# Hybrid streaming encoder on one core: memory values with tokens on partitions, a priority for the output projection, another slot for the last rows of x

## The chip, the cores and the metric

The kernel runs on one core of a Trainium2 chip. Its time is the device time of one launch in microseconds (us). TensorE (PE in the profile) multiplies, VectorE (DVE) and ScalarE (ACT) do elementwise work and read PSUM, GpSimd (POOL) does a little elementwise work, and SyncE (SP) issues nearly all DMAs, in the order of its own queue. Each engine works through its instructions in an order that is fixed when the kernel is built.

## What is computed

One layer of an encoder, for 1024 prompt tokens and 64 sample tokens, D = 1024:

- h = RMSNorm(x) @ W_in, split into the inputs of four mixers: a convolution of 31 taps over 256 channels, two kinds of softmax-like attention (`fox`, `sb`; 4 heads of 64 each) and a recurrence (`hgrn`).
- x += concat(convolution, fox, hgrn, sb) @ W_out.
- x += attention of 4 heads over 256 memory tokens, whose keys and values are made here: `mk = mem_prompt @ w_mk`, `mv = mem_prompt @ w_mv` (256 x 1024 by 1024 x 1024 each; both are outputs too).
- x += relu(RMSNorm(x) @ W_up)^2 @ W_down, then a last RMSNorm.

Activations and weights are float32. Each product is made as three products of float32r parts: a high part times a high part, high times low, low times high.

## The kernel before

**Layout.** Activations are kept with features on partitions and tokens in columns. A weight tile of 128 output columns is loaded as 8 blocks of 128 x 128 (`fetch_w`, L177: 512 KB), split on ScalarE into a high part `wh` and on VectorE into a low part `wl` (`split`, L169), and is the stationary operand of 8 x 3 products per chunk of tokens (`mm3`, L188). Tokens come in chunks of 512, 256 and 320 columns in the first stage (`CH`, L215) and in two groups afterwards (`GR`, L216): group 0 is tokens 0 to 511, group 1 the other 576, in chunks of 320 and 256.

**Preamble (L244 to L293).** The rows of x arrive as nine tiles `xt0` to `xt8` (L252); the ninth holds x_sample. TensorE transposes them in three rounds into `px`, from which the parts of h are made (`hx`, `ap`), and `stats` (L259) makes the scale `rb` of each token. The tiles xt7 and xt8 stand in slots that attention uses later: xt7 in that of `vn`, xt8 in that of `kT`.

**Mixing stage (L296 to L1032).** Four generators ("lanes") emit instructions: the projections with W_in, attention, convolution, recurrence. The loop at L1016 takes turns among them, and each lane has a priority: `PR_PROJ`, `PR_ATT`, `PR_HGRN`, `PR_CONV`, in this order from first to last. A scheduler sets the order on each engine when the kernel is built: among the instructions that it takes to be ready it puts the one with the lowest priority number first. The products of the projections have the priority `PR_MM` (`products`, L322), later than all lanes, so that they fill what attention leaves of TensorE. The first lane follows `PROJ_ORDER` (L40); it begins with the first pair of `sb` heads, whose key is written into `kT` by `sink_k` (L439) and whose value goes through `sink_v` (L444). Sums are made in a pool of two PSUM banks (`ps_mm`, tag `mm`).

**Memory keys and values (`memory_kv`, L373)** are the last step of the first lane. The memory tokens are transposed into `mT`, split, and for each of the 8 tiles of 128 weight columns of w_mk and of w_mv one sum of 24 products with the 256 tokens as columns is made. `sink` (L389) copies it out (`mkvT`), for the keys stores it, transposes it back in two products (`pn`), copies that (`mnat`) and stores it with tokens in rows.

**Convolution (`lane_conv`, L758).** Three chunks of tokens, the last one from token 752 on. Its 31 taps for two halves of the channels are VectorE instructions (L794); then come mean and variance by products with ones (`pme`, `pva`), a normalization and a sigmoid, in two halves, and stores into `mix_d`.

**Output projection.** After the lanes the priority is `PR_END` (L1033). The eight mixer rows of group 0 are loaded into slots of `kT`, `vn` and `q2` (L1043 to L1047) and split (`split_mix`, L1035); then the pools of the mixing stage close. `dense_add(0, w_out, ...)` (L1227) runs over 8 weight tiles with 24 products of 512 columns each (`pa`) and adds the sums to `xt` (L1120). Its hook `ahead` (L1219) loads x and, at the second weight tile, loads and splits the eight mixer rows of group 1, convolution last. `rms_apply` makes h for group 0, and `dense_add(1, ...)` projects group 1, taking mixer rows 2 to 7 first and the convolution's rows 0 and 1 last (`MIX`, L1226). Memory attention, the feed-forward part and the last norm follow; the change does not touch them.

Of the kernel before, what the change touches and what calls it, by code (L numbers as in the profile page):

```python
# [8 lines left out]
F32 = mybir.dt.float32  # L9
F32R = mybir.dt.float32r  # L10
BF16 = mybir.dt.bfloat16
U8 = mybir.dt.uint8
AF = mybir.ActivationFunctionType
# [4 lines left out]
P = 128  # L18
D = 1024
KD = D // P  # L20
SP = 1024
SS = 64
T = SP + SS
# [5 lines left out]
NMEM = 256  # L29
# [9 lines left out]
P_COST = 18.0  # L39
PROJ_ORDER = "sb0 h0 sb1 ff cv fox0 h1 fox1 kv".split()  # L40

PR_PROJ, PR_ATT, PR_HGRN, PR_CONV, PR_MM, PR_END = (i * 10 ** 6 for i in (1, 2, 3, 4, 5, 10))


class Need:
# [7 lines left out]
def kernel(ctx: ExitStack, tc: tile.TileContext, *args):  # L53
    nc = tc.nc
# [12 lines left out]
    def rows(ap):  # L67
        return ap[0, 0].rearrange("t h d -> t (h d)")

    def mm(out, lhsT, rhs, start, stop, **kw):  # L70
        nc.tensor.matmul(out, lhsT=lhsT, rhs=rhs, start=start, stop=stop, **kw)  # L71

    def act(out, in_, func, **kw):
        nc.scalar.activation(out=out, in_=in_, func=func, **kw)  # L74
# [35 lines left out]
    for m in LEVELS[1:]:  # L110
        nb = 64 // m
        f = const.tile([P, nb], F32, name=f"lf{m}", tag="lvlf", bufs=1)
# [56 lines left out]
    def split(hi, lo, src):  # L169
        act(hi, src, AF.Copy)  # L170
        V.tensor_tensor(out=lo, in0=src, in1=hi.bitcast(F32), op=ALU.subtract)  # L171
# [72 lines left out]
    with ExitStack() as pa:  # L244
        xa = pa.enter_context(tc.tile_pool(name="xa", bufs=1))
        ps_a = pa.enter_context(tc.tile_pool(name="ps_a", bufs=4, space=PSUM))
        ss = xa.tile([P, 9], F32, name="ss")
        V.memset(ss, 0.0)
        junk = att.tile([P, 2, D], BF16, name="junk", tag="vn")
        xt = []  # L250
        for i, (t0, n) in enumerate(TT):
            xt.append((att.tile([P, T], F32, name=f"xt{i}", tag=("vn", "kT")[i - 7], bufs=(2, 1)[i - 7])[:, :D] if i >= 7 else  # L252
                       xa.tile([P, D], F32, name=f"xt{i}")))
            nc.sync.dma_start(out=xt[i][:n], in_=x_prompt[t0:t0 + n] if i < 8 else x_sample)
            if i in (3, 6):
                c = (C_SK, C_SV)[i // 3 - 1]
                early[c] = fetch_w(w_in, 0, KD, c)

        def stats(c0, cn, tiles):  # L259
            for i in tiles:  # L260
                n = TT[i][1]
                if i % 2:
                    V.tensor_tensor_reduce(out=junk[:n, 1], in0=xt[i][:n], in1=xt[i][:n], scale=1.0, scalar=0.0,
                                           op0=ALU.mult, op1=ALU.add, accum_out=ss[:n, i:i + 1])
                else:
                    act(junk[:n, 0], xt[i][:n], AF.Square, accum_out=ss[:n, i:i + 1])
            r = rstd_chain(xa, len(tiles), ss[:, tiles[0]:tiles[0] + len(tiles)], "ra", scale=1.0 / D)
            pr = ps_a.tile([P, 512], F32, name="pr", tag="pr", bufs=1)
            for j, i in enumerate(tiles):
                n = TT[i][1]  # L270
                dg = xa.tile([P, P], F32, name="dg", tag="dg", bufs=2)
                V.tensor_scalar(out=dg[:n, :n], in0=ident[:n, :n], scalar1=r[:n, j:j + 1], scalar2=None, op0=ALU.mult)
                mm(pr[:, j * P:j * P + n], ones[:n], dg[:n, :n], True, True)
            act(rb[:, c0:c0 + cn], pr[:, :cn], AF.Copy)

        for c0, cn in CH:
            tiles = [i for i, (t0, n) in enumerate(TT) if c0 <= t0 < c0 + cn]
            for k in range(KD):
                px = ps_a.tile([P, 512], F32, name="px", tag="px")
                for i in tiles:  # L280
                    t0, n = TT[i]
                    nc.tensor.transpose(px[:, t0 - c0:t0 - c0 + n], xt[i][:n, k * P:(k + 1) * P], ident[:n, :n])
                hi, lo = h_at(k, c0, cn)
                act(hi, px[:, :cn], AF.Identity, scale=g_mix[:, k:k + 1])
                V.scalar_tensor_tensor(out=lo, in0=px[:, :cn], scalar=g_mix[:, k:k + 1], in1=hi.bitcast(F32),
                                       op0=ALU.mult, op1=ALU.subtract)
                xs = xa.tile([P, 512], F32, name="xs", tag="xs", bufs=4)
                if k % 2:
                    V.tensor_copy(out=xs[:, :cn], in_=px[:, :cn])
                else:  # L290
                    act(xs[:, :cn], px[:, :cn], AF.Copy)
                nc.sync.dma_start(out=xT_d[:, k, c0:c0 + cn], in_=xs[:, :cn])
            stats(c0, cn, tiles)  # L293
# [20 lines left out]
    def flush():  # L314
        if pending[0]:
            pending[0]()
        pending[0] = None

    def project(c0, sink, src=w_in, moving=h_at, chunks=CH):
        together([(c0, sink)], src, moving, chunks)  # L320
# [52 lines left out]
    def memory_kv():  # L373

        mT = [pair0() for _ in range(KD)]
        for i in range(2):
            mt = wp.tile([P, KD, P], F32, name="mt", tag="wr")
            nc.sync.dma_start(out=mt, in_=mem_prompt[i * P:(i + 1) * P].rearrange("p (k c) -> p k c", k=KD))
            for kb in range(2):
                ps = ps_mm.tile([P, 4, P], F32, name="psmt", tag="mm")  # L380
                for k in range(4):
                    nc.tensor.transpose(ps[:, k], mt[:, 4 * kb + k], ident)
                for k in range(4):
                    split(*(t[:, i * P:(i + 1) * P] for t in mT[4 * kb + k]), ps[:, k])

        def memory(k, t0, n):
            return mT[k][0][:, :n], mT[k][1][:, :n]

        def sink(out, m, is_k):  # L389
            def run(ps, j):  # L390
                s = wk.tile([P, 512], F32, name="mkvT", tag="st")
                act(s[:, :NMEM], ps, AF.Copy)
                if is_k:
                    nc.sync.dma_start(out=mkT_d[m], in_=s[:, :NMEM])

                def later():
                    pn = ps_mm.tile([P, 4, P], F32, name="pn", tag="mm")
                    for i in range(2):
                        nc.tensor.transpose(pn[:, i], s[:, i * P:(i + 1) * P], ident)
                    d = wk.tile([P, 4, P], F32, name="mnat", tag="nat")  # L400
                    act(d[:, :2], pn[:, :2], AF.Copy)
                    nc.sync.dma_start(out=rows(out).rearrange("(i p) c -> p i c", p=P)[:, :, m * P:(m + 1) * P],
                                      in_=d[:, :2])
                return later
            return run

        for src, out in ((w_mk, mk_p), (w_mv, mv_p)):
            for m in range(KD):
                project(m * P, sink(out, m, src is w_mk), src, memory, [(0, NMEM)])
                yield 0.25  # L410
        flush()

    def spill(slot):
        def sink(ps, j):
# [601 lines left out]
    while lanes:  # L1016
# [13 lines left out]
            ln.need = y.key  # L1030
        else:
            ln.t += y * ln.rate  # L1032
    tc.cur_priority = PR_END  # L1033

    def split_mix(k, src, t0, n, which):  # L1035
        nc.sync.dma_start(out=src, in_=mix_d[k][:, t0:t0 + n])
# [63 lines left out]
    def rms_apply(g, gains, rr, which, over=False):  # L1100

        dst = [pair(which) for _ in range(KD)]
        for c0, cn in GR[g][2]:
            for k in range(KD):
                hf = normed(g, k, gains, rr, c0, cn, xT[g][k] if over else None)
                split(dst[k][0][:, c0:c0 + cn], dst[k][1][:, c0:c0 + cn], hf[:, :cn])
        return dst

    def dense_add(g, src, r0, kt, a, psum, ahead=None, store=False, after=None, order=None):

        t0, n, _ = GR[g]
        for m in (0, 4, 1, 5, 2, 6, 3, 7) if after else range(KD):
            w = load_w(src, r0, kt, m * P)
            if ahead:
                ahead(m)
            for c0, cn in GR[g][2]:
                ps = psum.tile([P, 512], F32, name="pa", tag="mm")
                mm3(ps[:, :cn], w, lambda k: (a[k][0][:, c0:c0 + cn], a[k][1][:, c0:c0 + cn]), kt, order=order)
                xs = xT[g][m][:, c0:c0 + cn]
                V.tensor_tensor(out=xs, in0=xs, in1=ps[:, :cn], op=ALU.add)  # L1120
            if store:
                nc.sync.dma_start(out=x2_d[m][:, t0:t0 + n], in_=xT[g][m])
            if after:
                tc.cur_priority += 600
                after(m)
                tc.cur_priority -= 600
# [3 lines left out]
    with ExitStack() as pm_:  # L1130
# [94 lines left out]

        MIX = (2, 3, 4, 5, 6, 7, 0, 1)  # L1226
        dense_add(0, w_out, 0, KD, mix[0], ps1, ahead)  # L1227
        h2 = rms_apply(0, g_mem, rms_stats(0, ps2, "sc"), 0)
        dense_add(1, w_out, 0, KD, mix[1], ps1, lambda m: load_x(1, m), order=MIX)
        for g in range(2):  # L1230
# [321 lines left out]
```

## Time and profile before

| | us |
|---|---|
| median of 3 runs | 1765.38 |
| lowest and highest run | 1765.11, 1768.04 |
| profiled execution | 1760.05 |
| span of its instructions | 1758.3 |
| TensorE busy | 1694.8 |
| VectorE busy | 1172.1 |
| ScalarE busy | 791.4 |
| GpSimd busy | 94.1 |
| mean granted TensorE clock | 0.991 |

The profile is of one execution, whose own time is 1760.05 us; its span runs from the first to the last instruction. Busy times of one engine are shares of that span; they overlap between engines. Matmuls are pipelined: the duration of a single one is longer than the distance between two in a row, so the cost of many is read from a run of them.

### The profile page before, as it was taken

What the parts mean: (1) busy time and instruction counts of PE and PEld (TensorE: products, weight loads), DVE (VectorE), ACT (ScalarE), POOL (GpSimd) and SP (SyncE); (2) the same over time, 40 slices, a digit from 0 to 9 for tenths busy, and PEclk for the clock granted to TensorE, in tenths of its full rate; (3) what the DMA queues carried; (4) which work ended last, traced back from release to release, by engine and by line L of the source; (5) the groups of instructions that cost most, each with busy time, mean ns of one, the idle gap of its engine ahead of it and who ended that gap; (6) DMA issues with size and microseconds to landing.
All of it is one profiled execution on the core that took longest, in us unless ns stands there. A gap on an engine that the chain in (4) does not pass through costs nothing.

```text
span 1758.3 us, 29395 instructions
## 1 busy us (share of the span) xinstructions
PE 1694.8 (96%) x11379; PEld 1504.8 (86%) x11379; DVE 1172.1 (67%) x2231; ACT 791.4 (45%) x1614; POOL 94.1 (5%) x201
## 2 busy tenths in 40 slices
PE   6999999999989979999999999999999999999997
PEld 4987768787777768988899989999999999999987
DVE  6266789988986897667777696555556444444435
ACT  6265657547447855346456363433334212122213
POOL 3021111101120200000000000000000000000000
PEclk9999999999999989999999999999999999999999
DMA  8521332242237348232522343333335722332112
GB/s 256 142 80 33 111 87 88 71 123 76 71 95 215 111 140 254 73 97 67 156 78 73 101 124 99 99 106 99 101 105 203 266 94 87 99 100 74 37 37 102
DMA packets 233195, 194.70 MB, mean 111 GB/s; under 512 B 17502, under 2 KB 199711, under 8 KB 233055
## 3 DMA queue, kind: packets, MB, share of 16 engines
q1 hardware_dynamic: 232639, 192.54, 35.6%
q8 instruction: 90, 1.47, 0.4%
q14 instruction: 50, 0.41, 0.1%
q10 hardware_dynamic: 160, 0.26, 0.0%
q0 software_dynamic: 256, 0.01, 0.0%
HBM read 137.96 MB, written 53.72 MB: 109 GB/s over the span
## 4 chain that ended last, share of the span: by engine, by line
PE 75%; DVE 15%; ACT 4%; DMA 3%; issue 2%; POOL 0%; SPq 0%; DVEq 0%; POOLq 0%; ACTq 0%
PE pz L71 24%; PE pw L71 15%; PE pm L71 11%; PE pa L71 9%; PE pq L71 5%; PE z L71 2%; DVE y L794 2%; PE pmo L71 2%; PE pms L71 1%; PE po L71 1%; PE pt L517 1%; PE pv L71 1%; DVE wl L171 1%; DVE hsc L934 1%; DVE sba L494 1%
## 5 line engine op out<-in xcount | busy, mean ns | idle before, releaser
L74 ACT ACTIVATE wh<-wr 128x1024 fp32r<-128x1024 f32 (+1 forms) x179 | 161.4, 909 | 439.6 <-PE pz L71 195.2
L171 DVE TENSOR_TENSOR wl<-wr,wh 128x1024 fp32r<-128x1024 f32 (+1 forms) x179 | 184.3, 1036 | 63.8 <-ACT wh L74 62.5
L71 PE MATMUL pw<-ap,wh 128*128 128x512 f32 x720 | 223.3, 391 | 1.0 <-DVE xt L1120 0.6
L71 PE MATMUL pz<-ap,wh 128*128 128x288 f32 x988 | 198.3, 294 | 0.0
L71 PE MATMUL pa<-ap,wh 128*128 128x256 f32 (+2 forms) x768 | 187.0, 332 | 2.1 <-DVE xt L1120 2.1
L71 PE MATMUL pm<-hx,wh 128*128 128x512 f32 (+1 forms) x640 | 176.6, 363 | 2.1 <-ACT wh L74 1.4
L71 PEld LDWEIGHTS pz<-ap,wh 128*128 128x128 f32 x988 | 161.3, 188 | 4.6
L71 PE MATMUL pm<-ap,wh 128*128 128x256 f32 (+1 forms) x768 | 164.7, 307 | 0.0
L71 PEld LDWEIGHTS pw<-ap,wh 128*128 128x128 f32 x720 | 130.0, 188 | 23.5 <-issue 0.8
L71 PE MATMUL pz<-ap,wl 128*128 128x288 f32 x494 | 145.4, 294 | 0.0
L71 PEld LDWEIGHTS pa<-ap,wh 128*128 128x128 f32 x768 | 132.3, 191 | 12.5 <-DVE xt L1120 2.4
L71 PE MATMUL pw<-ap,wl 128*128 128x512 f32 x360 | 140.3, 390 | 0.0
L71 PEld LDWEIGHTS pm<-hx,wh 128*128 128x128 f32 x640 | 110.2, 192 | 20.6 <-ACT wh L74 2.2
L71 PEld LDWEIGHTS pm<-ap,wh 128*128 128x128 f32 x768 | 123.8, 191 | 4.2 <-issue 1.7
L71 PE MATMUL pa<-ap,wl 128*128 128x512 f32 (+2 forms) x384 | 127.2, 332 | 0.1
L1349 DVE TENSOR_TENSOR xt<-xt,pz 128x576 f32<-128x576 f32 x56 | 42.2, 753 | 115.6 <-PE pz L71 108.8
L71 PE MATMUL pm<-ap,wl 128*128 128x256 f32 (+1 forms) x384 | 114.0, 297 | 0.0
L71 PE MATMUL pm<-hx,wl 128*128 128x512 f32 (+1 forms) x320 | 112.7, 352 | 0.1
L794 DVE SCALAR_TENSOR_TENSOR y<-ext,cwT,y 128x376 f32<-128x376 f32 (+1 forms) x180 | 100.9, 604 | 0.3
L1349 DVE TENSOR_TENSOR xt<-xt,pw 128x512 f32<-128x512 f32 (+2 forms) x80 | 51.0, 638 | 69.8 <-PE pw L71 67.6
L71 PE MATMUL pq<-ap,wh 128*128 128x512 f32 (+2 forms) x384 | 93.0, 331 | 0.0
L71 PEld LDWEIGHTS pz<-ap,wl 128*128 128x128 f32 x494 | 92.7, 188 | 0.0
(385 smaller groups left out, 3572.9 us busy)
## 6 DMA issues: line engine op xcount, KB each, us to landing
wr<-in_w_up_dram SPq DMA_DIRECT2D x32, 512.0 KB, 4.1
wr<-in_w_down_dram SPq DMA_DIRECT2D x32, 512.0 KB, 3.5
wr<-in_w_in_dram SPq DMA_DIRECT2D x24, 512.0 KB, 4.3
hid_d<-ap SPq DMA_DIRECT2D x32, 288.0 KB, 2.4
aq<-hid_d SPq DMA_DIRECT2D x32, 288.0 KB, 3.7
wr<-in_w_out_dram SPq DMA_DIRECT2D x16, 512.0 KB, 4.2
wr<-in_w_mq_dram SPq DMA_DIRECT2D x16, 512.0 KB, 3.8
wr<-in_w_mo_dram SPq DMA_DIRECT2D x32, 256.0 KB, 2.8
```

What stands on the lines that cost most here:

```text
L71: nc.tensor.matmul(out, lhsT=lhsT, rhs=rhs, start=start, stop=stop, **kw)
L74: nc.scalar.activation(out=out, in_=in_, func=func, **kw)
L171: V.tensor_tensor(out=lo, in0=src, in1=hi.bitcast(F32), op=ALU.subtract)
L494: V.tensor_tensor_scan(out=v[:, ::-1], data0=z[:, n - 1:0:-1], data1=v[:, ::-1], initial=-NEG, op0=ALU.add, op1=ALU.subtract)
L517: nc.tensor.transpose(ps[:w, j - jb], p[:, j * P:j * P + w], ident)
L794: V.scalar_tensor_tensor(out=y, in0=ext[:, j:j + n], scalar=cwT[:, ct, j:j + 1], in1=y, op0=ALU.mult, op1=ALU.add)
L934: V.copy_predicated(sc[r, s_at:s_at + ng, :, r].rearrange("p g h (c w) -> p (g h) c w", w=2 * m)[:, :, :, m:], lvl[m][r, par * nb:(par + 1 ...
L1349: eng.tensor_tensor(out=out, in0=a, in1=b, op=ALU.add)
```

## The change

- Memory values: the 256 memory tokens become the stationary operand, 128 at a time, and the weights move, 512 columns at a time. A half of the columns of w_mv (512) is loaded in four tiles of 256 rows; two PSUM banks, one for each 128 tokens, are summed over all four tiles, 12 products of 512 columns for each tile, and copied out as rows of tokens. There are no transposes and no `mkvT` for the values. The keys are made as before.
- The output projection's preparations and its first group get a priority of their own, `PR_OUT`, between the recurrence and the convolution; `PR_END` begins after that group's products.
- The tile for x_sample stands in the slot of `q2` (the queries) and no longer in that of `kT`.

```diff
-PR_PROJ, PR_ATT, PR_HGRN, PR_CONV, PR_MM, PR_END = (i * 10 ** 6 for i in (1, 2, 3, 4, 5, 10))
+PR_PROJ, PR_ATT, PR_HGRN, PR_OUT, PR_CONV, PR_MM, PR_END = (i * 10 ** 6 for i in (1, 2, 3, 4, 5, 6, 10))
...
-            xt.append((att.tile([P, T], F32, name=f"xt{i}", tag=("vn", "kT")[i - 7], bufs=(2, 1)[i - 7])[:, :D] if i >= 7 else
-                       xa.tile([P, D], F32, name=f"xt{i}")))
+            xt.append(att.tile([P, T], F32, name="xt7", tag="vn")[:, :D] if i == 7 else
+                      att.tile([P, 2, T], F32, name="xt8", tag="q2", bufs=1)[:, 0, :D] if i == 8 else
+                      xa.tile([P, D], F32, name=f"xt{i}"))
...
-        for src, out in ((w_mk, mk_p), (w_mv, mv_p)):
-            for m in range(KD):
-                project(m * P, sink(out, m, src is w_mk), src, memory, [(0, NMEM)])
+        for m in range(KD):
+            project(m * P, sink(mk_p, m), w_mk, memory, [(0, NMEM)])
+            yield 0.25
+        flush()
+
+        for h in range(2):
+            cols = slice(h * 512, (h + 1) * 512)
+            ps = [ps_mm.tile([P, 512], F32, name="pmv", tag="mm") for _ in range(2)]
+            for k0 in range(0, KD, 2):
+                raw, hi, lo = (wp.tile([P, KD, P], dt, name=nm, tag=nm).rearrange("p (k m) c -> p k (m c)", k=2)
+                               for nm, dt in (("wr", F32), ("wh", F32R), ("wl", F32R)))
+                nc.sync.dma_start(out=raw, in_=w_mv[k0 * P:(k0 + 2) * P, cols].rearrange("(k p) c -> p k c", p=P))
+                split(hi, lo, raw)
+                prio, tc.cur_priority = tc.cur_priority, PR_MM + pending[1]
+                for i in range(2):
+                    for k in range(2):
+                        mh, ml = (t[:, i * P:(i + 1) * P] for t in mT[k0 + k])
+                        for j, (x, w) in enumerate(((mh, hi), (ml, hi), (mh, lo))):
+                            mm(ps[i], x, w[:, k], k0 + k + j == 0, k0 + k == KD - 1 and j == 2)
+                pending[1] += 24
+                tc.cur_priority = prio
                 yield 0.25
-        flush()
+            for i in range(2):
+                d = wk.tile([P, 512], F32, name="mvn", tag="nat")
+                act(d, ps[i], AF.Copy)
+                nc.sync.dma_start(out=rows(mv_p)[i * P:(i + 1) * P, cols], in_=d)
...
-    tc.cur_priority = PR_END
+    tc.cur_priority = PR_OUT
...
         dense_add(0, w_out, 0, KD, mix[0], ps1, ahead)
+        tc.cur_priority = PR_END
         h2 = rms_apply(0, g_mem, rms_stats(0, ps2, "sc"), 0)
```

The sink of the keys keeps its copy, its store and its two transposes; only the test `is_k` goes.

## Rows read from the trace of the kernel before

**Rows 1.** The page: busy time of TensorE; its busy tenths in 40 slices.

```profile
PE 1694.8 (96%) x11379; PEld 1504.8 (86%) x11379; DVE 1172.1 (67%) x2231; ACT 791.4 (45%) x1614; POOL 94.1 (5%) x201
...
PE   6999999999989979999999999999999999999997
```

**Rows 2.** Table by stretch: length, busy of each engine (instructions), clock, DMA share, GB/s.

```profile
100.00:640.00 540.00, 515.11 (x3976) 423.85 (x3975) 448.44 (x926) 339.02 (x761) 74.52 (x131) 1.00 0.35 98
600.00:640.00 40.00, 39.97 (x338) 33.71 (x337) 35.95 (x71) 28.65 (x56) 0.00 (x0) 1.00 0.40 118
...
651.00:653.00 2.00, 0.00 (x0) 0.00 (x0) 2.00 (x5) 0.00 (x0) 0.00 (x0) 0.50 0.41 160
...
641.00:701.00 60.00, 50.75 (x242) 41.49 (x242) 49.32 (x92) 28.46 (x57) 0.00 (x0) 0.91 0.72 229
```

**Rows 3.** Chain that ended last, 641 to 701 us: start, length, what.

```profile
641.45 11.30 DVE y L794 x23
...
661.45 0.62 PE pva L71 x4
...
662.07 39.14 PE pa L71 x172
```

**Rows 4.** Timeline of TensorE, 643 to 702 us: start, length, instruction, idle before.

```profile
643.60 1.20 PE L71 MATMUL pa<-ap,wh 128*128 128x512 f32 x4
653.90 1.59 PE L71 MATMUL pme<-y,ones 128*128 128x183 f32 x4 [9.11 <-DVE cvo L805]
...
701.26 0.45 PE L71 MATMUL pa<-ap,wh 128*128 128x320 f32 x2
```

**Rows 5.** Timeline of VectorE, 641 to 683 us.

```profile
641.88 11.31 DVE L794 SCALAR_TENSOR_TENSOR y<-ext,cwT,y 128x366 f32<-128x366 f32 x22
...
654.38 1.21 DVE L171 TENSOR_TENSOR wl<-wr,wh 128x1024 fp32r<-128x1024 f32 x1
...
658.65 0.68 DVE L171 TENSOR_TENSOR ap<-mix,ap 128x512 fp32r<-128x512 f32 x1
...
682.04 0.75 DVE L171 TENSOR_TENSOR ap<-aq,ap 128x576 fp32r<-128x576 f32 x1
```

**Rows 6.** DMA issues: ns min/median/max, first and last start; and one of SP's timeline.

```profile
L1036 SPq DMA_DIRECT2D mix<-mix_d x8: 320/404/460, 500.2 to 621.0; - x8
...
L179 SPq DMA_DIRECT2D wr<-in_w_out_dram x16: 367/378/411, 626.8 to 734.4; - x16
...
676.97 0.79 SPq L1036 DMA_DIRECT2D aq<-mix_d x2
```

**Rows 7.** Timeline and table by stretch around the first evacuations of keys and values.

```profile
36.36 0.69 DVE L447 TENSOR_TENSOR vT<-pm,rb 128x512 f32<-128x512 f32 x1
...
43.89 0.67 DVE L441 TENSOR_TENSOR kT<-pm,rb 128x512 f32<-128x512 f32 x1
...
47.03 0.78 PE L71 MATMUL pm<-ap,wh 128*128 128x256 f32 x2
...
36.00:46.00 10.00, 6.95 (x36) 4.72 (x35) 7.65 (x22) 6.51 (x16) 0.19 (x1) 0.86 0.56 188
47.00:50.00 3.00, 3.00 (x16) 3.00 (x15) 0.69 (x1) 0.97 (x2) 1.84 (x3) 0.51 0.72 187
```

**Rows 8.** By tile: transposes of x, loads into q2 (ns min/median/max, first to last).

```profile
L282 PE MATMUL px<-ident,xt x72: 270/273/477, 5.7 to 41.6; 128*128 128x128 f32 x64, 64*128 64x64 f32 x8
...
L540 SPq DMA_DIRECT2D q<-q_d x16: 445/586/963, 78.1 to 546.9; - x16
```

**Rows 9.** By tile: copies of memory sums; transposes in a row; chain: products of 256, of 512 columns.

```profile
L74 ACT ACTIVATE mkvT<-pm x16: 365/384/387, 543.5 to 641.9; 128x256 f32<-128x256 f32 x16
...
639.01 0.60 PE L517 MATMUL pt<-ident,fp 128*128 128x128 f32 x4
...
282.53 2.87 PE pm L71 x24
...
1367.30 2.73 PE pw L71 x12
```

More of the change, by code (lines that the diff above doesn't have):

```diff
@@ L387, in memory, with sink @@
             return mT[k][0][:, :n], mT[k][1][:, :n]
-        def sink(out, m, is_k):
+        def sink(out, m):
             def run(ps, j):
@@ L392, in run @@
                 act(s[:, :NMEM], ps, AF.Copy)
-                if is_k:
-                    nc.sync.dma_start(out=mkT_d[m], in_=s[:, :NMEM])
+                nc.sync.dma_start(out=mkT_d[m], in_=s[:, :NMEM])
                 def later():
```

## The prediction

> **What bounds the kernel now.** I read four views. The page's busy table says that TensorE is the engine of this kernel: 96% of the span, and in its 40 slices TensorE is at 9 but for four, among them the first (to 44 us) at 6 and the fifteenth (615 to 659 us) at 7 [rows 1]. So a gain has to come from a stretch where TensorE sits idle, or from TensorE work that disappears. The table by stretch says where. From 100 to 640 us TensorE is busy 515 of 540 us with VectorE at 448; from 600 to 640 it is busy all the time. From 651 to 653 it does nothing at all, while VectorE is busy in all of it, and the granted clock has fallen to 0.50, the lower of its two levels (1.2 of 2.4 GHz) [rows 2]. The chain of waits names the work in that hole: 23 convolution taps of VectorE, 11.3 us [rows 3]. The timelines of the two engines show why. The projection has begun at 643.60 with four products and stops; the next thing in TensorE's order, a sum of the convolution, waits 9.11 us for VectorE, and the projection's own next product needs `wl`, whose subtraction stands on VectorE behind 22 taps and starts at 654.38 [rows 4, 5]. The taps belong to tokens from 752 on, and the first group's projection reads only tokens below 512: it waits for work that it does not need. The order is one of priority: both the projection and its splits carry PR_END, the convolution PR_CONV, which comes first. A second, smaller hole is at the start: 40 to 50 us.
>
> **Part 1, the projection's own priority.** PR_OUT stands ahead of PR_CONV and PR_MM. Nothing is added or removed; the splits of the mixer rows (4 of the 8 low halves come after 653, 0.68 us each [rows 5]), the low half of the first weight tile (1.21 us) and the additions into `xt` go ahead of the taps on VectorE. Their data lie ready: the eight mixer rows were loaded between 500 and 621 us, the first w_out tile was issued at 626.8 [rows 6]. These 3.9 us of VectorE then lie beside attention's last products.
> What it can give: between the first product at 643.60 and the first product of the second group at 701.26 [rows 4] lie 57.7 us. The work there is 8 x 24 = 192 products of 512 columns at 39.14/172 = 0.2276 us [rows 3], 43.7 us, and 16 products of the convolution's sums, four times 0.62 us [rows 3], 2.5 us: 46.2 us. At most 11.5 us can go (most of it the idle time, the rest the half clock behind it).
> What it costs: the taps do not vanish, they are late next. From 641 to 701 VectorE has 49.3 us of work [rows 2]; in a stretch shortened to 48.6 us it is full, and the convolution, last in priority, ends near its end. In the trace of before the time from the end of the taps (653.2) to the load of the finished rows (676.97) is 24 us, and the first of them is split 6 later (to 682.8) [rows 5, 6]. If the taps share VectorE with the projection's 22 us (weights 8 x 1.21, splits 4 x 0.68 and 6 x 0.75 [rows 5], and 8 additions taken like the splits of their size, 8 x 0.68), they end some 20 us after the projection's start (ten of their own, ten of the rest) and the rows are split at 50. The second group's projection wants them at 46 plus what it can do without: it takes mixer rows 0 and 1 last, so three banks take 18 products each of 256 or 320 columns, about 7 us. Need 53, ready 50: no stall by this estimate. If all 22 us of that work went ahead of the taps, they would end at 32 and the rows be ready at 62, a stall of 9 us. Bounds 2.5 to 11.5; I take 10.5, near the upper end, since the estimate leaves 3 us of slack and TensorE has been kept full everywhere else where such a filler competes [rows 2].
> SP's queue is passed too: the x loads and w_out loads move ahead of the convolution's stores, and issue takes 0.3 to 0.5 us each [rows 6]; SP is otherwise idle there. The `xt` loads write where the staged rows lay, so they start when these are split, as now; three banks, 16 us of products, cover them.
>
> **Part 2, the last rows of x.** The first evacuation into `kT` waits for the last transposes that read x_sample from that slot (41.6 us [rows 8]): the value's evacuation ran at 36.36, the key's only at 43.89 [rows 7], though its products were older. Then the key's transposes and chunk 1's products (47.03) follow, at the lower clock. In `q2`'s slot the x rows hold up nobody: the first load into q2 is at 78.1 [rows 8]. So the key's evacuation can follow the value's, and products fill the holes. What is there to be had: TensorE is busy 6.95 of the 10 us from 36 to 46, so 3.05 idle; and from 47 to 50, at the lower clock, it works for 3 us on what takes half as long at the upper, 1.5 us [rows 7]. Bounds 0 and 4.6 us; a loss I exclude, as the slot's next user comes 36 us later. I take 3.0: the transposes still pace part of it. TensorE is nearly full afterwards [rows 2], so this carries on.
>
> **Part 3, memory values.** Removed: 8 x 24 = 192 products of 256 columns at 2.87/24 = 0.1196 us (23.0 us), 16 transposes at (0.60-0.27)/3 = 0.11 us (one alone 0.27, four in a row 0.60; 1.8 us), 8 copies `mkvT` of 0.38 us and 8 `mnat` of the same size on ScalarE. Added: 96 products of 512 columns at 2.73/12 = 0.2275 us (21.8 us), 4 copies of 512 columns, at most twice the 0.38. Equal: eight weight tiles of 512 KB with their splits. [rows 9] TensorE saves 1.2 + 1.8 = 3.0 us, ScalarE some 3 us, which is off the path.
> The rows thus say that a product costs its columns at 2.4 GHz plus 13 to 14 ns at either width. The Trainium skill (TensorE: Matmul & The Clock Gate, Back-to-back issue gap) puts the fixed part of an isolated product at 2.5 ns; by that the wider products would save 0.2 us instead of 1.2 and the sum would be 1 us smaller. The trace disagrees here, and I go by its rows.
> Both banks of the pool now hold sums through four weight tiles; at the end of a half two copies (at most 1.5 us) stand between the last product and the next. Attention's products are there to cover that; the second time it stands ahead of the output projection. Bounds -1 and 3.0; I take 2.0, as TensorE is full in the stretch where these products lie [rows 2].
>
> **Sum.** 10.5 + 3.0 + 2.0 = 15.5 us. The profiled execution took 1760.05 us (span 1758.3), 5.3 below the median of the runs shown: it would become 1744.6, and the median 1765.4 becomes 1749.9. Said as 1750.
>
> **Rivals.**
> A. The convolution becomes the wait inside the projection. For it: VectorE has 49.3 us of work for 48.6, and a product of the convolution's sums stood at the head of TensorE's order for 9.11 us until VectorE delivered [rows 4]. The Trainium skill (same page, What happens when you issue a matmul) says that only weight loads are pulled ahead while products stay in program order, which the row does not contradict; so a sum placed too early stops the projection. Against: low priority puts them late. Price 9 us: 2.5 + 3 + 2 = 7.5, time 1757.9.
> B. The mixing stage keeps its length, because VectorE and the chain of attention set its end, not TensorE: parts 2 and 3 give nothing. For: 448 of 540 us of VectorE; against: TensorE at 515 [rows 2]. 10.5 us, time 1754.9.
> C. Slower: SP's queue. The loads of the second group's mixer rows 0 and 1 are traced at the projection's second tile; if they are queued there, they wait for the convolution's stores (44 us after the start by the estimate above), with the w_out loads behind them. Tiles for four steps are there, 22 us of products; the next would land and be split some 6 us later, as the mixer rows are, at 50 us: a stall of 28 us. Against 16.5 us of gains that loses 11.5: 1776.9. It decides from a stall of 16.5 us on. Against it: before, the same two loads were queued behind the stores, at 676.97 [rows 6].
> D. The priority does nothing for the taps' place, because the splits are taken as ready only after them; and of the 5 us of parts 2 and 3 half arrives: 1762.9.
>
> **How the numbers follow.** Forecast 0.58 (own range 1746.3, where every upper bound holds, to 1754), A 0.14, B 0.14, C 0.06, D 0.08. The runs of before spread over 2.9 us; below 1746.3 that gives 1743.4, say 1743. Upwards the range takes in B and A with the same spread, to 1760; C and D, 0.14, are left out. Forecast, A and B are faster by over 0.2% (3.5 us, about what a measurement here can tell from no change): 0.86. D is within it, C slower.
>
> **What would show it.** Right: no idle stretch of TensorE over 2 us between attention's last `pv` and the first w_out product; clock 1.00 there; taps of VectorE running beside `pa` products; first group's projection in 46 to 48 us; key evacuation before 38 us and the 47 us products gone from the lower clock; half as many products and 16 fewer transposes for w_mv. Wrong: a wait of `pa` on conv rows, or of `pme` on VectorE, of several us; w_out loads issued behind waiting loads; or a mixing stage whose end has not moved 4 to 5 us apart from the hole.

## The result and the profile after

The kernel with the change took 1756.59 us (median of 4 runs, 1754.32 to 1758.60) beside 1766.14 us of the kernel before: ratio 0.9944, 95% interval [0.9927, 0.9962]. Measured once more, in five rounds beside experiments, it took 1754.95 us, ratio 0.9963 [0.9950, 0.9976]. So it is faster, by 9.9 us in the first measurement and by 6.5 us in the second; 15.5 us were forecast. The profiled execution took 1757.08 us (span 1755.4).

First the page: TensorE's busy time, and its busy tenths in 40 slices, as in [rows 1].

```profile
PE 1690.2 (96%) x11254; PEld 1495.0 (85%) x11267; DVE 1173.5 (67%) x2231; ACT 788.3 (45%) x1602; POOL 98.1 (6%) x201
...
PE   7999999999998999899999999999999999999997
```

The first slice went from 6 to 7, and the hole in the fifteenth (615 to 659 us) is a 9 now. But two slices further on, the seventeenth (702 to 746 us), has fallen to 8: a new hole. TensorE is busy for 4.6 us less than before.

The table by stretch (length, busy time of each engine with its instructions, clock, DMA share, GB/s) answers to [rows 2, 7]:

```profile
36.00:46.00 10.00, 10.00 (x72) 8.19 (x71) 7.85 (x23) 7.40 (x18) 0.00 (x0) 1.00 0.68 225
47.00:50.00 3.00, 3.00 (x25) 2.99 (x24) 0.58 (x2) 0.04 (x1) 0.00 (x0) 1.00 0.71 186
...
641.00:703.00 62.00, 55.52 (x262) 47.15 (x262) 44.16 (x83) 22.42 (x44) 0.00 (x0) 0.96 0.61 196
700.00:720.00 20.00, 12.85 (x76) 12.06 (x77) 15.08 (x26) 13.29 (x25) 0.00 (x0) 0.74 0.42 124
```

At the start TensorE is busy in all 10 us (6.95 before), and from 47 to 50 its clock is 1.00 (0.51 before). From 700 to 720 us it works for 12.85 of 20 us, and its mean clock there is 0.74. VectorE's timeline shows what changed at the start:

```profile
35.63 0.69 DVE L462 TENSOR_TENSOR kT<-pm,rb 128x512 f32<-128x512 f32 x1
...
36.76 0.69 DVE L468 TENSOR_TENSOR vT<-pm,rb 128x512 f32<-128x512 f32 x1 [0.38 <-PE pm L71]
```

The key's evacuation into `kT`, at 43.89 before and behind the value's, now comes first. The next chunk's products start at 39.2 us instead of 47.03.

The chain that ended last, from the projection on (start, length, what), answers to [rows 3]:

```profile
642.78 45.44 PE pa L71 x192
...
703.64 2.75 DMA aq<-mix_d
...
707.15 5.43 PE pa L71 x23
```

All 192 products of the first group run in one piece: from the first of them to the first of the second group are 45.8 us (688.54), where 57.7 were. That is the gain that part 1 was after, 11.9 us. But then the chain goes over a DMA that fetches finished convolution rows at 703.64. TensorE's timeline shows the idle time before its instructions in brackets:

```profile
642.78 0.95 PE L71 MATMUL pa<-ap,wh 128*128 128x512 f32 x2 [2.60 <-ACT mvn L74]
...
688.04 0.78 PE L71 MATMUL pme<-y,ones 128*128 128x183 f32 x4
...
691.12 0.78 PE L71 MATMUL pme<-y,ones 128*128 128x183 f32 x4
...
707.15 1.43 PE L71 MATMUL pa<-ap,wh 128*128 128x320 f32 x4 [8.85 <-ACT ap L74]
```

There are two new waits. The large one stands at 707.15: the second group waits 8.85 us for rows of the convolution to be split. The reason stands 19 us further up: the convolution's sums `pme`, at 653.90 before and in front of all but four of the projection's products, now stand at 688.04, behind the last of the 192 products. VectorE, which is to deliver to them, was not the one that was late:

```profile
670.77 0.74 DVE L826 COPY cvo<-pco 30x256 f32<-30x256 f32 x2
...
677.36 0.69 DVE L1141 TENSOR_TENSOR xt<-xt,pa 128x512 f32<-128x512 f32 x1 [3.35 <-PE pa L71]
...
682.80 0.69 DVE L1141 TENSOR_TENSOR xt<-xt,pa 128x512 f32<-128x512 f32 x1 [3.34 <-PE pa L71]
...
688.24 0.69 DVE L1141 TENSOR_TENSOR xt<-xt,pa 128x512 f32<-128x512 f32 x1 [3.35 <-PE pa L71]
688.86 0.60 DVE L837 SCALAR_TENSOR_TENSOR y<-pme,y 128x183 f32<-128x183 f32 x2
```

The taps and the copy behind them are done at 671.5. From there on VectorE idles three times for 3.3 us, since it waits for `pa`, while the sums that its finished taps feed stand on TensorE behind those very `pa`. Then the norm takes its time. On SP's timeline the first finished rows are stored at 696.71, and the two that the second group lacks are loaded at 703.64:

```profile
696.71 0.82 SPq L853 DMA_DIRECT2D mix_d<-y  x2
...
703.64 1.23 SPq L1057 DMA_DIRECT2D aq<-mix_d  x2
```

The small new wait, 2.60 us ahead of the first product, is one of ScalarE's queue. Its timeline:

```profile
638.86 0.60 ACT L74 ACTIVATE mvn<-pmv 128x512 f32<-128x512 f32 x1 [0.53 <-PE pmv L71]
641.19 1.06 ACT L74 ACTIVATE wh<-wr 128x1024 fp32r<-128x1024 f32 x1 [1.72 <-DMA wr<-in_w_out_dram]
642.15 0.58 ACT L74 ACTIVATE mvn<-pmv 128x512 f32<-128x512 f32 x1
```

The second copy of the memory values stands behind the high half of a w_out tile that is still on its way (1.72 us of waiting for the DMA). The projection's first product waits for that copy. So although attention's last `pv` starts at 634.9 (643.4 before), the projection starts at 642.78, only 0.8 us earlier than before [rows 4].

The books of the two profiled executions: start of the projection 0.8 us earlier, first group 11.9 us shorter, second group up to the first query product 10.2 us longer (688.54 to 755.0 against 701.26 to 757.5). 2.5 us are left there, and 2.9 in the span. The timed runs show more, 6.5 and 9.9 us: executions of the kernel before lie between 1758.8 and 1768.4 us, and its profiled one, 1760.05, is a short one.

### The profile page after: what moved, and what is told of

It reads as the page before. It is cut to its first block, busy times and chain, and to the rows that moved or that the text cites. A ratio compares the mean times of both kernels' runs of the same rounds, so it can differ in the third digit from the quotient of the medians.

```text
span 1755.4 us, 29149 instructions
## 1 busy us (share of the span) xinstructions
PE 1690.2 (96%) x11254; PEld 1495.0 (85%) x11267; DVE 1173.5 (67%) x2231; ACT 788.3 (45%) x1602; POOL 98.1 (6%) x201
## 4 chain that ended last, share of the span: by engine, by line
PE 77%; DVE 11%; ACT 5%; DMA 4%; issue 2%; POOL 1%; SPq 0%; DVEq 0%; POOLq 0%; ACTq 0%
PE pz L71 25%; PE pw L71 16%; PE pm L71 10%; PE pa L71 9%; PE pq L71 5%; PE z L71 2%; PE pmo L71 2%; PE pms L71 1%; PE pt L538 1%; DVE hsc L955 1%; PE pv L71 1%; PE po L71 1%; DVE sba L515 1%; DVE y L815 1%; DVE wl L171 1%
## 5 line engine op out<-in xcount | busy, mean ns | idle before, releaser
L71 PE MATMUL pm<-hx,wh 128*128 128x512 f32 (+1 forms) x512 | 150.0, 378 | 3.2 <-ACT wh L74 1.5
L1371 DVE TENSOR_TENSOR xt<-xt,pz 128x576 f32<-128x576 f32 x56 | 42.2, 754 | 116.7 <-PE pz L71 112.2
L71 PEld LDWEIGHTS pm<-hx,wh 128*128 128x128 f32 x512 | 89.4, 190 | 21.3 <-ACT wh L74 2.1
L71 PE MATMUL pm<-hx,wl 128*128 128x512 f32 (+1 forms) x256 | 93.9, 367 | 0.2 <-DVE wl L171 0.2
```

The source lines that it names most:

```text
L1371: eng.tensor_tensor(out=out, in0=a, in1=b, op=ALU.add)
```

## The experiments

The theory: all three parts do on TensorE what they say, but the new priority puts the convolution's sums behind the projection on TensorE too, and the rows come late. The rivals: VectorE is too full to make them earlier; or the parts at the start and in the memory values bring nothing.

**The yardstick and the three parts alone.** First the kernel before, unchanged.

> The kernel before, unchanged, as a measure of how far two executions of one kernel lie apart, since its profiled execution (1760.05 us) was 5 to 8 us shorter than its timed ones and the changed kernel's was not. Theory: a ratio of 1.000 within 0.002, and a profile in which the hole before the output projection (9.11 us of TensorE idle) and the first key evacuation (43.9 us) stand where they stood. Rival, that the short execution had another course: one of the two holes is larger by some 5 us.

1762.95 us, ratio 0.9997 [0.9987, 1.0007]; its profiled execution took 1759.76 us. What can be told here is some 0.1%, and a single profiled execution can stand 3 us and more off the median.

The tile of x_sample alone:

```diff
-            xt.append((att.tile([P, T], F32, name=f"xt{i}", tag=("vn", "kT")[i - 7], bufs=(2, 1)[i - 7])[:, :D] if i >= 7 else
+            xt.append(att.tile([P, T], F32, name="xt7", tag="vn")[:, :D] if i == 7 else
+                      att.tile([P, 2, T], F32, name="xt8", tag="q2", bufs=1)[:, 0, :D] if i == 8 else
```

> Only the last rows of x in the queries' slot. Theory: the key is evacuated before 38 us, TensorE is busy from 36 to 46 us, everything behind it comes 3 to 4 us earlier (first pv product at 103.5 instead of 107.5) and the end moves by 3 us, 1763. Rival, that the mixing stage absorbs it because VectorE and the attention chain set its end: first projection product unmoved at 643.6, time 1766.

1757.10 us, ratio 0.9966 [0.9953, 0.9979], that is 6.0 us (3.7 to 8.3). This one edit gives most of what the whole change gives. The first row below is of its table by stretch, the second of TensorE's timeline:

```profile
36.00:46.00 10.00, 10.00 (x66) 7.93 (x65) 7.87 (x22) 7.67 (x20) 0.00 (x0) 1.00 0.67 212
```

```profile
651.04 1.59 PE L71 MATMUL pme<-y,ones 128*128 128x183 f32 x4 [9.11 <-DVE cvo L806]
```

The early hole is closed; the hole in the projection is as before, 9.11 us, only the whole stage lies earlier: first product 640.7 (643.6 before, 645.0 in the second execution of that kernel), first query product 753.7 (757.5 and 758.0). So what is won at 45 us does reach the end.

The priority alone:

```diff
-    tc.cur_priority = PR_END
+    tc.cur_priority = PR_OUT
...
+        tc.cur_priority = PR_END
```

> Only the output projection's own priority. Theory: the hole of 9.1 us before the projection is gone, but the convolution's sums stand on TensorE behind all 192 products of the first group, so its last rows come some 28 us later than before and the second group waits about 9 us for them: net 2 us, 1764. Rival, the prediction's forecast that the rows come in time beside the projection: no wait over 2 us in the second group, net 10.5 us, 1755.5.

1760.26 us, ratio 0.9984 [0.9975, 0.9992]: 2.8 us (1.4 to 4.4), not the 10.5 of the forecast. TensorE's timeline has the same pattern as that of the full change, without its other two parts:

```profile
688.36 0.78 PE L71 MATMUL pme<-y,ones 128*128 128x183 f32 x4
...
707.16 1.43 PE L71 MATMUL pa<-ap,wh 128*128 128x320 f32 x4 [8.55 <-ACT ap L74]
```

The old hole is gone and the new wait is there. The priority itself brings it.

The memory values alone (the part of the diff in `project`'s callers, from `sink` to the store of `mvn`):

> Only the memory values with tokens on partitions. Theory: TensorE has 3 us less work in a stretch where it is full, so the first product of the output projection comes 2 to 3 us earlier and the time is 1763.5. Rival, that both banks held through four weight tiles cost what the products save: first projection product at 643 to 645, time 1766 to 1767.

1764.24 us, ratio 1.0006 [0.9996, 1.0016]: at best 0.7 us of gain, none in the middle. TensorE's timeline ahead of and in the projection:

```profile
644.64 0.73 PE L71 MATMUL pa<-ap,wh 128*128 128x512 f32 x2 [0.69 <-ACT mvn L74]
...
647.50 1.22 PE L71 MATMUL pa<-ap,wh 128*128 128x512 f32 x2 [2.13 <-ACT wh L74]
...
657.64 1.59 PE L71 MATMUL pme<-y,ones 128*128 128x183 f32 x4 [8.91 <-DVE cvo L825]
```

Attention ends earlier (last `pv` 637.5, 643.4 before), but the products of w_mv lie singly among attention's and run on to 643.6; then ScalarE's copies and splits make TensorE wait 0.69 and 2.13 us. The wait that ends last in this stage is the long one behind them, 8.91 us for the taps. VectorE's timeline shows these:

```profile
640.51 16.42 DVE L814 SCALAR_TENSOR_TENSOR y<-ext,cwT,y 128x366 f32<-128x366 f32 x32
```

Here 32 taps stand in one run and end at 656.9; in the kernel before it was 23, which ended at 653.2 (654.6 in its second execution). So as long as the hole is open, VectorE sets its end, and what the part saves TensorE ahead of it cannot be seen behind it. The kernel with the old values and a closed hole, below, is the better test of this part.

By their ratios the three parts alone are worth 6.0, 2.8 and -1.1 us, 7.7 together; the whole is worth 6.5 to 9.9. Within their intervals, one to two us each way, they add up: no loss between the parts shows. What is missing is missing in part 1 and in part 3; part 2 gave more than forecast.

**The convolution's sums ahead of the projection.** The changed kernel once more, and with one edit, in the same rounds:

```diff
+            if last:
+                tc.cur_priority = PR_OUT - 5 * 10 ** 5
```

It stands in `lane_conv`, ahead of the norm: for the convolution's last stretch of tokens, the sums, the norm and the stores rank ahead of the projection. The taps stay behind it.

> The changed kernel again, in more rounds, since its ratio came from four runs each. Theory: the parts add up (0.9966, 0.9984 and 1.0006 alone give 0.9956), ratio 0.994 to 0.996. Rival, that they hinder one another: over 0.997; or help: under 0.993. In the profile the second group waits again about 9 us for the convolution's rows.

> The changed kernel, in which the convolution's last normalization (sums, VectorE and ScalarE steps) gets a priority ahead of PR_OUT while its taps stay behind it. Theory, that the sums stood on TensorE behind all 192 products although VectorE had the taps ready at 671: the sums now run between the products, the rows are stored before 690, the 8.85 us wait in the second group and the half clock behind it go, 8 us less than the changed kernel, ratio 0.990. Rival, that VectorE is what makes the rows late (rival A as the prediction priced it): the rows come at about 700 as before and the time does not move.

The changed kernel: 1754.95 us, ratio 0.9963, with the waits of 8.82 us (conv rows) and 2.60 us (`mvn`) as before. The edited one: 1751.29 us, ratio 0.9944 [0.9932, 0.9956], 3.7 us less. Its last group of `pme` runs at 673.23 instead of 688.84, and the rows are loaded at 690.53 instead of 701.36; of the wait for them 1.1 us are left. The first row below is of TensorE's timeline, the second of SP's:

```profile
673.23 0.81 PE L71 MATMUL pme<-y,ones 128*128 128x183 f32 x4
```

```profile
690.53 0.99 SPq L1059 DMA_DIRECT2D aq<-mix_d  x2
```

So the order on TensorE was the cause, and VectorE could deliver in time. The edit also ranks the norm's steps on VectorE and ScalarE earlier, but that is not where the time came from: from the first of these sums to the load pass 21.8 us here (668.77 to 690.53), beside 15.6 in the changed kernel (685.78 to 701.36). But 8 us were to be had, and 3.7 came. The table by stretch shows where the rest went:

```profile
710.00:720.00 10.00, 7.16 (x54) 6.90 (x53) 10.00 (x18) 7.38 (x11) 0.00 (x0) 1.00 0.09 28
720.00:730.00 10.00, 8.37 (x40) 7.93 (x40) 5.98 (x9) 0.68 (x1) 0.00 (x0) 0.66 0.44 132
```

and TensorE's timeline:

```profile
719.80 0.50 PE L71 MATMUL pa<-ap,wh 128*128 128x256 f32 x2 [2.84 <-DVE xt L1143]
...
722.47 0.64 PE L71 MATMUL pa<-ap,wl 128*128 128x320 f32 x1 [1.11 <-DVE wl L171]
```

From 710 to 720 VectorE is busy all the time and TensorE waits for it. On VectorE's timeline the work there is the norm ahead of the memory attention (`tm<-xt,g_mem,tm` and the splits into `ap`), which the program writes before the second group's projection and which goes ahead of that projection's additions. Afterwards TensorE's clock is down.

**The memory values' products.** Two more edits of the same place: the twelve products of a tile set close together (the first keeps its rank, the eleven others rank ahead of everything else), and the values as in the kernel before but with the other two parts and the early norm.

```diff
+                            tc.cur_priority = 5 * k0
```

> The changed kernel, in which the 12 products of each tile of w_mv stand in one run on TensorE, as the products with w_mk do. Theory, that the values' products lost their saving by being scattered singly among attention's products: mixing stage 1 to 2 us shorter, first projection product at 640 to 641 instead of 642.8, ratio 0.001 below the changed kernel's. Rival, that the wait of the first sum's copy behind a w_out split on ScalarE is all: the copy now stands ahead of that split, the 2.6 us go, but TensorE's products end where they ended.

1756.65 us (1751.12 to 1761.09), ratio 0.9972 [0.9960, 0.9984], no better than the changed kernel. The products of w_mv now end at 632.3, and the wait for `mvn` is gone. But attention is pushed back: its last `pv` is at 649.0, behind the first of the projection's products (640.85), TensorE idles 2.28 us for attention's `fp` instead, and the wait for the conv rows is 8.8 us. Here work moved ahead of attention only delays attention. (The profiled execution, 1760.30 us, is one of the long ones.)

> The kernel of e4_norm_first with the memory values made as before: what the values' part is worth where both holes are closed and the end of TensorE's work in the mixing stage counts directly. Theory: the values give 0 to 2 us, so this one is equal to e4 or up to 2 us slower. Rival, that they cost: this one is faster than e4 by 1 to 2 us.

1751.84 us, ratio 0.9947 [0.9935, 0.9959], beside 0.9944 with the new values: the values' part is worth nothing that can be told, in both surroundings. With the old values TensorE does not idle ahead of the projection, and its clock stays at 1.00 there; the projection starts at 641.2, 1.1 to 1.5 us later than with the new ones (640.1 and 639.7), and yet the first query product comes at 749.6, not later than theirs (750.0 and 750.2). The new values' 2.5 and 2.4 us of idle time and the low clock behind it take what their products save.

**The two waits that are left.** Four kernels in the same rounds: the one with the early norm again as the yardstick, and two edits on top of it, singly and together.

> The version with the second group's convolution norm ahead of the projection's products, once more, as the yardstick for the three kernels beside it: a ratio of 0.993 to 0.9957 as before (0.9944), with about 2.8 us of TensorE waiting for VectorE's sum into x near 717 us and about 2.5 us of TensorE waiting for the memory values' copy near 640 us.

1751.67 us, ratio 0.9941 [0.9930, 0.9953], with both waits. Its waits of TensorE from 600 to 760 us (total, times, longest):

```profile
PE pa L71 <- DVE xt L1143: 3.4, 2, 2.8
PE pa L71 <- ACT mvn L74: 2.4, 1, 2.4
PE pa L71 <- DVE wl L171: 1.1, 1, 1.1
...
```

The copies of the memory values on VectorE:

```diff
-                act(d, ps[i], AF.Copy)
+                V.tensor_copy(out=d, in_=ps[i])
```

> The copies of the memory values out of PSUM go from ScalarE to VectorE, all else as in the yardstick. Theory (the 2.5 us of idle TensorE ahead of the projection are ScalarE's queue: the second copy stands behind a split that waits for a DMA): the wait for mvn falls below 0.5 us, the projection starts some 2 us earlier, and the time falls by 1.5 to 2.5 us against the yardstick. Rival (VectorE is as late there, or the projection's products are set by their own weights): the wait moves to a weight split or to VectorE, the start moves by less than 0.7 us, and the time stays within 0.7 us of the yardstick's.

```profile
PE pa L71 <- ACT ap L74: 5.3, 1, 5.3
PE pme L71 <- DVE cvo L826: 2.0, 1, 2.0
PE pa L71 <- DVE mvn L431: 1.3, 1, 1.3
...
```

1752.49 us, ratio 0.9950 [0.9937, 0.9963]: no gain, so the expectation that followed from the queue was a miss. The wait did shrink, from 2.4 to 1.3 us. But VectorE is the engine with the taps: in this trace 33 taps stand behind the projection's first product, 28 in the yardstick's, the sums wait 2.0 us for them, and the rows come 5.3 us late. (This profiled execution, 1756.71 us, is the longest of its five; the trace of the last kernel below, with the same copies, has the same three waits.)

The norm ahead of the memory attention behind the second group's additions:

```diff
-        h2 = rms_apply(0, g_mem, rms_stats(0, ps2, "sc"), 0)
+        rr = rms_stats(0, ps2, "sc")
+        tc.cur_priority += LATER
+        h2 = rms_apply(0, g_mem, rr, 0)
+        tc.cur_priority -= LATER
```

Only `rms_apply` moves. The sum of squares on TensorE stays where it was: with a later rank it would, by its place in the order, stand behind all of the second group's products, the same mistake again; that was not run.

> The norm of the first group ahead of the memory attention (16 multiplications and 16 splits of 128x512) gets a later priority than the second group's projection, so that VectorE takes the projection's sums into x first. Theory (what the early convolution norm won is given back between 710 and 722 us because VectorE is full there with this norm): the wait of pa for x, 2.8 us and 3.4 us in all, and the 1.1 us for a weight split are gone, TensorE's clock stays at 1.00 from 710 to 740 us, and the first query product comes 4 to 6 us earlier, 3 to 5 us less time than the yardstick. Rival (the norm itself is needed by then): the query products wait for it, and the time is the yardstick's within 1 us or above it.

```profile
PE pa L71 <- ACT mvn L74: 2.2, 1, 2.2
PE pa L71 <- ACT ap L74: 1.6, 1, 1.6
PE pva L71 <- ACT sq L74: 0.6, 1, 0.6
PE pme L71 <- DVE cvo L826: 0.3, 1, 0.3
```

1746.67 us (1745.43 to 1748.23), ratio 0.9913 [0.9900, 0.9926]: 5.0 us less than the yardstick, and the fastest of all. The waits for `xt` and `wl` are gone, and the table by stretch shows VectorE as full as before but TensorE without a hole and with its clock at 1.00:

```profile
710.00:720.00 10.00, 10.00 (x79) 10.00 (x78) 10.00 (x18) 5.82 (x9) 0.00 (x0) 1.00 0.54 159
720.00:730.00 10.00, 10.00 (x77) 10.00 (x76) 10.00 (x16) 4.89 (x8) 0.00 (x0) 1.00 0.23 70
```

VectorE was not too slow there; it did the wrong thing first.

> Both edits at once: the copies of the memory values on VectorE and the later norm ahead of the memory attention. If the two waits are separate and in one chain, the time falls by the sum of the two, some 5 to 7 us below the yardstick (about 1744 to 1746 us beside a yardstick of 1751). Rival (they hide one another, or the earlier start only makes the second group wait for its convolution rows): no lower than the better of the two by more than 1 us.

1751.11 us, ratio 0.9945 [0.9932, 0.9959], 4.4 us more than without the copies on VectorE. The wait for conv rows is back (4.6 us) and so is that of the sums for the taps (2.1). The two edits do not add up.

One measure puts these runs side by side: the time from the projection's first product to the first query product, by the starts in each trace. It leaves out where the stage begins, which differs by up to 2.3 us between two executions of one kernel. The measure itself differs by up to 0.9 us between two executions (rows "again"), so smaller differences say nothing.

| kernel | from | to | us |
|---|---|---|---|
| before | 643.60 | 757.5 | 113.9 |
| before, again | 645.0 | 758.0 | 113.0 |
| x_sample's tile alone | 640.7 | 753.7 | 113.0 |
| values alone | 644.64 | 761.2 | 116.6 |
| priority alone | 644.4 | 756.0 | 111.6 |
| the change | 642.78 | 755.0 | 112.2 |
| the change, again | 640.5 | 753.1 | 112.6 |
| with the early norm | 640.1 | 750.0 | 109.9 |
| with the early norm, again | 639.69 | 750.2 | 110.5 |
| early norm, values as before | 641.2 | 749.6 | 108.4 |
| early norm, later `h2` | 642.08 | 744.4 | 102.3 |

The last one is 11.6 us below the first, about what the hole held. Three places had to be ranked for it, not one. Whether the ranks alone, without the other two parts of the change, would give as much is not shown: no such kernel was run.

## Why the prediction was right and wrong

The side was right, the range of 1743 to 1760 holds the time, and the place of the hole and its cause were read rightly. Of 15.5 us that were forecast 6.5 to 9.9 came. That the range holds the time is luck in part: 1756.6 lies above the forecast's own range (1746.3 to 1754), and the range reaches it only because it was widened for rivals A and B and for the spread of the runs. Two misses also offset one another: by the timed runs of the parts alone, parts 1 and 3 gave 10.8 us less than taken, part 2 gave 3.0 more.

**Part 1, what it can give: right.** The hole went as read, 57.7 us to 45.8, beside the 46 to 48 forecast, with taps running beside the products. The 45.8 hold only 4 of the 16 sums that the forecast counted in; the other 12 moved into the second group.

**Part 1, what it costs: the step that failed.** It costed the convolution's delay on VectorE alone, and took the 24 us from the end of the taps to the load of the rows from the trace of before. There TensorE stood waiting for the sums. With the new priority it has something else to do first: the load came 32.1 us after the copy behind the taps was done (671.5 to 703.64), and of these 16.5 went by before the first of the last sums ran on TensorE (688.04); the other 15.6 are less than the 24 taken. The taps took longer as well, to 28 us after the projection's start and not 20: 28 of them were left at that start, some 14.5 us, and not ten. "Need 53, ready 50" became need 55.5 (698.3, where TensorE ran dry) and ready 64.4 (707.1), after the first product at 642.78. Of the part's 10.5 us 2.8 came, near the lower bound of 2.5. In the kernel with the early norm, where the sums do not stand behind the products, need and ready nearly meet: TensorE ran dry 55.2 us after the projection's start (695.3), the two rows were split 55.5 and 57.7 us after it, and 1.1 us of waiting was left. The sentence "Against: low priority puts them late" in rival A held the error: late on TensorE was taken for harmless.

**Part 2: right in its mechanism, small in its size.** 3.0 us taken, bounds 0 and 4.6; the timed runs give 6.0 (3.7 to 8.3), the profiled execution 3.0 (1760.05 to 1757.09). Products filled the hole and the lower clock went. Why the timed runs gain more than the profiled ones is open; the kernel before scatters more (1759.56 to 1768.40, in 29 runs) than the one with this edit (1755.09 to 1757.55, in only 5).

**Part 3: wrong.** 2.0 us taken; none measured, at best 0.7 alone. The step "Attention's products are there to cover that" failed at the end of the second half. The two copies at the end were named, with the place; but their cost was taken as their own length, at most 1.5 us, without what stands between them on ScalarE: a split that waits for its DMA. The idle time was 2.60 us, and behind it the 192 products took 45.44 us instead of the 43.7 of the forecast, because TensorE's clock was down for some of them: 4.3 us in all against 3.0 saved by the forecast's count.

**The rivals.** A came true in its place, in its price and nearly in its time (9 us priced, 8.85 us of idle time; 1757.9 priced, 1756.59 measured). Its reason, VectorE full, did not: VectorE idled while the sums stood in TensorE's queue, and a kernel that changes only their rank, and that of the norm behind them, lost most of the wait. So that the price fits is luck. That products stay in program order, for which rival A cited the Trainium skill (TensorE: Matmul & The Clock Gate, What happens when you issue a matmul), agrees with the trace: the sums ran in the build's order behind 192 products while their data lay ready from 671.5 on. The forecast just looked for a sum placed too early, and it was placed too late. B is refuted for part 2 (the start moved, and the end with it); for part 3 nothing arrived, in the changed kernel because of a new wait; in the kernel with the values alone VectorE's taps set the end of the hole, which is near B's reason. C did not occur: SP stores the rows at 696.71 and loads at 703.64, and the wait is for the rows. D is refuted, the taps moved.

**What it named as signs.** Of those for "right", the early key evacuation, the clock at 47 us, half the products for w_mv, 16 fewer transposes, taps beside `pa` products and the 45.8 us were there; the clock of 1.00 at the projection's start was not (0.50 from 644 to 646 us). Of those for "wrong", the wait of `pa` for conv rows was there, 8.85 us, and the idle stretch ahead of the projection was over 2 us.

## What to carry to other kernels

A priority holds on every engine that its instructions run on. Whoever lets a long run of products go first should look for the short products of the work that is passed over: a few sums that feed a long chain on other engines belong ahead of the run, even though their bulk belongs behind it. After each hole that closes, ask which work is next on the engine that is now full, and whether it is the work that is needed next; here the second and third rank were worth at least as much as the first (3.7 and 5.0 us beside 2.8). A copy put on a queue behind something that waits for a DMA costs that wait, not its own length.

## What the hardware showed that was not expected

How dear an idle stretch is depends on the clock behind it. In the changed kernel TensorE idled for 2.60 us ahead of the projection, and the granted clock was 0.50, the lower level (1.2 of 2.4 GHz), from 644 to 646 us; products of 512 columns took 0.43 us apiece there and 0.23 at the upper level. In the fastest kernel it idled for 2.17 us at the same place and the clock stayed at 1.00. These are the rows of the tables by stretch, the changed kernel first:

```profile
644.00:646.00 2.00, 2.00 (x6) 1.61 (x5) 2.00 (x6) 0.00 (x0) 0.00 (x0) 0.50 0.66 185
```

```profile
644.00:646.00 2.00, 2.00 (x10) 1.66 (x9) 2.00 (x5) 0.00 (x0) 0.00 (x0) 1.00 0.95 244
```

In the kernel with the early norm, TensorE idled three times between 717 and 722.5 us (2.84, 0.52 and 1.11 us), and 23 products of 320 columns then took 0.26 us apiece on the mean, up to 728.5 us, beside 0.15 before: some 2.7 us more, on top of 4.5 us of idle time.
